# A transformer block pair on one core: normed rows turned by transposes, splits and chain steps moved in the middle

## The chip, the cores and the metric

The kernel runs on one core of one Trainium2 chip, in one launch. The metric is the device time of an execution in microseconds (us); the times given are medians of runs. Its engines are TensorE (PE in the rows; PEld is its weight load, which runs beside it), VectorE (DVE), ScalarE (ACT), GpSimd (POOL) and SyncE (SP), which only issues DMAs here. Each engine takes its instructions in the order in which the program wrote them.

## The reference

The input is x, 256 tokens of 1024 features, float32. Two blocks follow one another.

The first block: h = rmsnorm(x) times the projections q, k, v, g_attn, x_lru, g_lru; differential attention over 8 heads (two softmaxes, their difference times v, a norm per head, a gate); a causal convolution and a gated linear recurrence on x_lru; both halves go through w_out, and x = x + rmsnorm(y).

The second block: a = rmsnorm(x) times the projections of two mixers. The first (hg) is a gated linear attention in chunks of 64 tokens. The second (nsa) has 8 query heads on 2 key heads and adds three attentions: over compressed keys (blocks of 32 keys, stride 16, through a small two-layer network), over selected blocks and over a window; with 256 tokens all blocks are selected. Both go through w_out and are added to x. Then a routed layer (peer): rmsnorm(x) times wq, scores against two sets of 128 keys, the best 16 of 16 x 16 pairs per head, and for the chosen experts gelu(u . x) weighted into v. All 16384 rows of u and of v are read. At the end a gate: x + (p @ ple_proj) * sigmoid(rmsnorm(x) @ ple_gate). Cut to what matters here:

```
def rmsnorm(x, g):
    return x * rsqrt(mean(x * x, axis=-1, keepdims=True) + 1e-6) * g

a    = rmsnorm(x, mix_norm)            # second block, its three norms
h    = x + concat(hgrn2(a), nsa(a)) @ w_out
h    = h + peer(rmsnorm(h, ffn_norm))
out  = h + (p @ ple_proj) * sigmoid(rmsnorm(h, ple_gate_norm) @ ple_gate)
```

## The kernel before

**Products.** A float32 matrix product is done as three products of rounded parts: every weight and every activation is split into a high part (a rounded copy) and a low part (the rest), and `three` (L294) adds high x high, high x low and low x high in PSUM. A weight unit is 128 x 1024 numbers. `Units` (L45) holds the order of all units: SyncE loads a unit into one of four raw buffers (L67), ScalarE copies the high part (L83), VectorE subtracts for the low part (L89; GpSimd does a share in some stages, L87). `ensure(m)` issues the splits up to unit m, but not past `U.limit`; `take` hands out a unit and looks two units ahead. A unit of class "s" gets one of three stream buffers, one of class "h" one of seven hold buffers, and a split waits until the products with the buffer's former unit are done. A raw buffer's next load waits for the low part.

**Order.** All orders are written by the program itself: each engine runs what was issued to it, in that order. The long chains (attention heads, norms, recurrences) are Python generators. `tick` (L259) adds 1.3 to a virtual clock and steps those that are due; a generator that yields 2.6 is stepped again two ticks later. Products call `tick` after every twelve products of 256 columns (`feat_unit`, L299) or six of 512. So a yield says how many products PE gets between one step of a chain and the next. It is no time of the chip.

**Stages around the change.** In `attention_head` (L622) scores, softmax, transposes of the weights (L666), their copy wT (L669) and the products with v (L675) follow one another; `head_pair_out` (L680) norms and gates two heads (ya, L701) and transposes them (L708). The eight units of g_lru and the first units of w_out run beside the last heads.

Then come the output products of the first block (`split_tokens`, L790): the last six units of w_out ("h") are run through for token half 0 and then for token half 1, so all six stay in hold buffers. Beside the products of half 1, half 0 goes through `post_chain` (L768: square sums, root, gain, sum with x) and `norm_chain` (L403). The norm squares its rows on ScalarE, takes the root with seven small VectorE operations, and multiplies a 128 x 128 identity by it (`diagonal`, L382). `turn` (L387) takes eight blocks of 128 x 128 of the rows as stationary operand and the diagonal as moving one, so that each product scales and transposes a block; ScalarE (L397) then evacuates the high parts and VectorE (L400) the low parts, with the gain. `after_o1` (L888) steps these chains and, in half 1, raises `U.limit` by one unit after each product. The query and key units (nq, nk; six, all "h") follow in the same way: half 0, `turn` of half 1, half 1, with `nsa_norm` (L949: square sums, reduction qss, root, qn, transposes L971) beside them.

In the second block's mixers, `compress` (L998), `forget_pair` (L1109: the scan G, then d1 and d2), `hgrn` (L1138), `nsa_cmp` (L1229) and `nsa_pair` (L1274) are such generators too; the first steps of nsa wait for the end of `compress`. Small products share four PSUM banks in turn (`sm_bank`, L137).

After w_out of the second block, `after_o2` (L1463) adds to x, squares, takes the root and the diagonal; `ffn_norm0` turns half 0, and half 1 is turned (L1519) after the small products of ple_proj, whose results ScalarE evacuates (L1515). The next products (wq, L1742) need both halves of x. `turn_ple` at the end uses `turn` with the plain identity.

Of the kernel before, what the change touches and what calls it, by code (L numbers as in the profile page):

```python
# [13 lines left out]
F32 = mybir.dt.float32  # L14
# [6 lines left out]
OP = mybir.AluOpType  # L21
# [83 lines left out]
def body(ctx: ExitStack, tc: tile.TileContext, I, out):  # L105
# [73 lines left out]
        U.add(("o1", k), I["w1_out"][k], cls="s" if n < 10 else "h")  # L179
    end1 = len(U.seq) - 6  # L180
    for u in range(4):
        U.add(("nq", u), I["w2_nq"][u], cls="h")
    for u in range(2):
        U.add(("nk", u), I["w2_nk"][u], cls="h")
    end1h = len(U.seq)
# [198 lines left out]
        nc.vector.tensor_scalar(dg, ident, r, None, op0=OP.mult)  # L384
        return dg

    def turn(tt, src, dg, x, gname, ks=range(KD)):  # L387

        lt = slice(tt * P, (tt + 1) * P)
        for k0 in range(ks[0], ks[-1] + 1, 2):  # L390
            pt = sm_bank("ps_n")
            for j in range(2):
                k = k0 + j
                nc.tensor.matmul(pt[:, j * P:(j + 1) * P], lhsT=src[:, tt, k * P:(k + 1) * P], rhs=dg, start=True, stop=True)
            for j in range(2):
                k = k0 + j
                nc.scalar.activation(x[0][:, k, lt], pt[:, j * P:(j + 1) * P], AF.Copy, scale=col(gname, k))  # L397
            for j in range(2):
                k = k0 + j
                nc.vector.scalar_tensor_tensor(x[1][:, k, lt], pt[:, j * P:(j + 1) * P], col(gname, k),  # L400
                                               x[0].bitcast(F32)[:, k, lt], op0=OP.mult, op1=OP.subtract)

    def norm_chain(tt, pool, gname, x, name, wait=0):  # L403

        ss = sums(name)
        for half in range(2):
            square_sum(ss, half, halves(res, tt)[half], pool)
        dg = diagonal(rsqrt_of_pair(ss, name), name)
        yield
        for _ in range(wait):  # L410
            yield
        turn(tt, res, dg, x, gname)


    U.limit = end1
# [206 lines left out]
    def attention_head(hd, pq, pair):  # L622

        yield 1.3
        qk = w1.tile([P, 2, T], F32, name="qk")
        nc.scalar.activation(qk, pq.rearrange("p (a b) -> p a b", b=T), AF.Copy)
        yield 2.6
        smx = w1.tile([P, 2, 384], F32, name="smx")
        mx = tiny.tile([P, 4], F32, name="mx")
        zs = tiny.tile([P, 4], F32, name="zs")  # L630
        pss = [sm_bank("ps_s0"), sm_bank("ps_s1")]
        for qb in range(2):
            kl = P * (qb + 1)
            for c in range(2):
                rows = slice(c * 64, c * 64 + 64)
                nc.tensor.matmul(pss[c][:, qb * P:qb * P + kl], lhsT=qk[rows, 0, qb * P:(qb + 1) * P],
                                 rhs=qk[rows, 1, :kl], start=True, stop=True)
        yield 1.3
        for qb in range(2):
            kl = P * (qb + 1)  # L640
            for c in range(2):
                nc.vector.tensor_tensor_reduce(smx[:, c, qb * P:qb * P + kl], pss[c][:, qb * P:qb * P + kl],
                                               causal[:, 256 - kl:], 1.0, NEG, OP.add, OP.max,
                                               accum_out=mx[:, 2 * c + qb:2 * c + qb + 1])
        nc.vector.tensor_scalar(mx, mx, -0.125, None, op0=OP.mult)
        yield 2.6
        for qb in range(2):
            kl = P * (qb + 1)
            for c in range(2):
                j = 2 * c + qb  # L650
                nc.scalar.activation(smx[:, c, qb * P:qb * P + kl], smx[:, c, qb * P:qb * P + kl], AF.Exp,
                                     bias=mx[:, j:j + 1], scale=0.125, accum_out=zs[:, j:j + 1])
        yield 2.6
        nc.vector.reciprocal(zs, zs)
        nc.vector.tensor_scalar(zs[:, 2:4], zs[:, 2:4], nlam, None, op0=OP.mult)
        wt = w1.tile([P, 384], F32, name="wt")
        for qb in range(2):
            kl = P * (qb + 1)
            cs = slice(qb * P, qb * P + kl)
            nc.vector.tensor_scalar(wt[:, cs], smx[:, 0, cs], zs[:, qb:qb + 1], None, op0=OP.mult)  # L660
            nc.vector.scalar_tensor_tensor(wt[:, cs], smx[:, 1, cs], zs[:, 2 + qb:3 + qb], wt[:, cs],
                                           op0=OP.mult, op1=OP.add)
        yield 2.6
        pt = sm_bank("ps_wt")
        for b in range(3):
            nc.tensor.transpose(pt[:, b * P:(b + 1) * P], wt[:, b * P:(b + 1) * P], ident)  # L666
        yield 1.3
        wT = w1.tile([P, 384], F32, name="wT")
        nc.scalar.activation(wT, pt[:, :384], AF.Copy)  # L669
        yield 1.3  # L670
        if not pair:
            pair.append(po_bank("ps_o"))
        po = pair[0][:, (hd % 2) * T:(hd % 2 + 1) * T]
        vc = slice(hd * P, (hd + 1) * P)
        nc.tensor.matmul(po[:, 0:P], lhsT=wT[:, 0:P], rhs=vt[:, 0, vc], start=True, stop=True)  # L675
        nc.tensor.matmul(po[:, P:2 * P], lhsT=wT[:, P:2 * P], rhs=vt[:, 0, vc], start=True, stop=False)
        nc.tensor.matmul(po[:, P:2 * P], lhsT=wT[:, 2 * P:3 * P], rhs=vt[:, 1, vc], start=False, stop=True)
        heads_done.append(hd)

    def head_pair_out(hp, pair):  # L680

        while not (2 * hp in heads_done and 2 * hp + 1 in heads_done):
            yield
        po = pair[0]
        sl = slice(2 * hp, 2 * hp + 2)
        osq = w1.tile([P, 512], F32, name="osq")
        nc.scalar.activation(osq, po, AF.Square)
        yield 1.3
        oss = tiny.tile([P, 4], F32, name="oss")
        nc.vector.tensor_reduce(oss, osq.rearrange("p (a b) -> p a b", b=P), axis=AX.X, op=OP.add)  # L690
        ors = rsqrt_of_sum(oss, 4, P, EPS, "or")
        yield 2.6
        while hp // 2 not in gates_rows:
            yield
        ya = w1.tile([P, NT, 2 * P], F32, name="ya")
        for j in range(2):
            hd = 2 * hp + j
            for qb in range(2):
                a = 2 * j + qb
                hs = slice(hd * P, (hd + 1) * P)  # L700
                nc.vector.scalar_tensor_tensor(ya[:, qb, j * P:(j + 1) * P], po[:, a * P:(a + 1) * P], ors[:, a:a + 1],  # L701
                                               gs[:, qb, hs], op0=OP.mult, op1=OP.mult)
        po_free.append(hp)
        yield 2.6
        py = sm_bank("ps_y")
        for j in range(2):
            for qb in range(2):
                nc.tensor.transpose(py[:, j * T + qb * P:j * T + (qb + 1) * P], ya[:, qb, j * P:(j + 1) * P], ident)  # L708
        yhv = flat(yh[:, sl])
        nc.scalar.activation(yhv, py, AF.Copy, scale=subg)  # L710
        yield 2.6
        nc.vector.scalar_tensor_tensor(flat(yl[:, sl]), py, subg, yhv.bitcast(F32), op0=OP.mult, op1=OP.subtract)
# [48 lines left out]
    hold_stack = rt.enter_context(ExitStack())  # L761
    hold = open_pool(hold_stack, "hold", 7, side="right")
    U.pools["h"] = (hold, 7, 2)
    U.limit = end1 + 7
    nrm = open_pool(hold_stack, "nrm2", side="right")
    pgb = nrm.tile([P, D], F32, name="post_g")
    nc.scalar.dma_start(pgb, I["post_g"].partition_broadcast(P))
# [120 lines left out]
    def after_o1(n, tt):  # L888
# [5 lines left out]
        else:  # L894
            if n == -1:
                next(ch[1])
            else:
                if n == 3:
                    finish(ch[0])
                if n == 5:  # L900
                    next(ch[1])
                if n == 0:
                    next(ch[0])
                U.limit += 1
                U.ensure(U.limit)

    split_tokens([("o1", k) for k in O1h],
# [13 lines left out]
    def after_nqk(n, tt):  # L921
        if tt == 0:
            if n == 0:
                next(ch[1])
            if n == 5:
                finish(ch[1])
                bq.append(po_bank("ps_nq"))
                bk.append(po_bank("ps_nk"))
                spawn(nsa_norm(0))
        else:  # L930
            tick()

    qT = b2.tile([P, 4, T], F32, name="qT")
# [64 lines left out]
    def compress(ps):  # L998
# [15 lines left out]
        for j in range(2):  # L1014
            for g in range(2):
                src = bass.AP(ksh.tensor, ksh[:, j, g, 0:1].offset, [list(ksh.ap[0]), [2, 16], [16, 15]])
                nc.vector.tensor_tensor(cinv[:, j, :, g, :], src, pec[:, j, :].unsqueeze(2).to_broadcast([P, 16, 15]), OP.add)
        yield 2.6
        h1T = cm.tile([64, 2, 2, 16], F32, name="h1T", bufs=1)
        nc.gpsimd.memset(h1T, 0.0)  # L1020
        yield from sm_wait(1)
# [87 lines left out]
    def forget_pair(np_, ps):  # L1109
# [7 lines left out]
        if np_ == 1:  # L1117
# [4 lines left out]
            nc.vector.tensor_tensor_scan(flat(G), flat(rst), flat(sg), 0.0, OP.mult, OP.add)  # L1122
            yield 2.6
            nc.vector.tensor_tensor(d1, G, G[:, :, 31:32].to_broadcast([P, 16, 64]), OP.subtract)
            nc.vector.tensor_tensor(d2, G[:, :, 63:64].to_broadcast([P, 16, 64]), G, OP.subtract)
            hg_ready["d"] = True

# [335 lines left out]
    def after_o2(half, tt):  # L1463
        add_half(res, tt, half, banks)
        square_sum(ss[tt], half, halves(res, tt)[half], w2, "osq2")
        if half:
            dgs[tt] = diagonal(rsqrt_of_pair(ss[tt], "n3%d" % tt), "n3")
            nc.scalar.dma_start(res_d[:, tt], res[:, tt])

    def ffn_norm0():  # L1470
# [1 line left out]
        after_o2(0, 0)  # L1472
        after_o2(1, 0)
        yield 6.5
        turn(0, res, dgs[0], x, "ffn")

    t_n0 = spawn(ffn_norm0())
    while not (1 in nsa_done and 1 in hg_done):
# [31 lines left out]
    for tt in range(NT):  # L1510
# [5 lines left out]
        nc.scalar.dma_start(pp_d[:, tt], pp[:, tt])  # L1516
        if tt == 0:
            U.ensure(U.done + 1)
    turn(1, res, dgs[1], x, "ffn")  # L1519
    pre.close()  # L1520


# [324 lines left out]
        U.ensure(U.done + 1)  # L1847

    def turn_ple(tt, half):
        turn(tt, res, ident, gT, "ple", range(4 * half, 4 * half + 4))  # L1850

    v_last(0, 0)
    v_last(0, 1)
# [113 lines left out]
```

## Time and profile before

| | us |
|---|---|
| median of 3 runs | 1233.61 (1228.92 to 1235.35) |
| the profiled execution's own time | 1229.46 |
| its span | 1227.7 |
| PE busy in the span | 1199.4 (98%) |
| VectorE busy | 914.7 (75%) |
| ScalarE busy | 632.6 (52%) |
| GpSimd busy | 149.8 (12%) |
| chain of work that ended last | PE 81%, VectorE 11%, ScalarE 4% |

The span is the profiled execution from its first to its last instruction; the own time is a little longer. PE's matmuls are pipelined and their ends are modelled, so a busy PE need not be at its peak. The first 100 us hold the first projections, 100 to 185 attention, 185 to 230 the first block's output, 230 to 405 the second block's mixers, and from 405 on the routed layer with its 256 units of u and v.

### The profile page before, as it was taken

How to read it: one execution, taken by the hardware profiler on the slowest of the kernel's cores; microseconds unless marked ns; L12 is line 12 of the kernel's file. 1: busy time of each engine (PE TensorE's matmuls, PEld its weight loads, DVE VectorE, ACT ScalarE, POOL GpSimd, SP SyncE). 2: the span in 40 equal slices, each digit the busy share in tenths (PEclk: the TensorE clock that was granted, in tenths of full speed). 3: DMA queues.
4: the chain of work that ended last, by engine and by line, in shares of the span. 5: the costliest groups of instructions: out<-in, count | busy, mean ns of one | idle time of the engine just before them, and what ended most of it. 6: DMA issues, size and time to landing. Idle time of an engine off the chain costs nothing.

```text
span 1227.7 us, 22587 instructions
## 1 busy us (share of the span) xinstructions
PE 1199.4 (98%) x8797; PEld 1081.2 (88%) x8797; DVE 914.7 (75%) x1964; ACT 632.6 (52%) x953; POOL 149.8 (12%) x231
## 2 busy tenths in 40 slices
PE   8999989899999999999999999999999999999998
PEld 8979988788887999999999999998888888888876
DVE  6799886758887689987887688788888555555544
ACT  6955665546664554545555444445444444444453
POOL 3410012000000577300000000000000000000061
PEclk9999999999999999999999999999999999999999
DMA  7464437353224756665555655555555675566561
GB/s 239 146 191 153 138 132 242 128 190 104 87 87 136 233 162 184 194 198 175 164 164 157 191 175 185 176 182 177 186 173 174 206 252 191 191 194 198 189 210 48
DMA packets 59083, 211.78 MB, mean 172 GB/s; under 512 B 6560, under 2 KB 7648, under 8 KB 58592
## 3 DMA queue, kind: packets, MB, share of 16 engines
q1 hardware_dynamic: 56736, 204.60, 52.5%
q10 hardware_dynamic: 2240, 5.75, 1.4%
q8 instruction: 69, 1.13, 0.4%
q14 instruction: 38, 0.31, 0.1%
HBM read 206.65 MB, written 3.15 MB: 171 GB/s over the span
## 4 chain that ended last, share of the span: by engine, by line
PE 81%; DVE 11%; ACT 4%; issue 2%; POOL 1%; DMA 1%; ACTq 0%; SPq 0%; DVEq 0%; POOLq 0%
PE ps_u L295 10%; PE ps_u L297 10%; PE ps_u L296 10%; PE ps_acc L295 9%; PE ps_acc L297 9%; PE ps_acc L296 9%; DVE los L89 3%; PE ps_w L1713 1%; PE ps_w L1714 1%; ACT his L83 1%; PE ps_pq L296 1%; PE ps_pq L297 1%; PE ps_pq L295 1%; PE ps_out L295 1%; PE ps_out L297 1%
## 5 line engine op out<-in xcount | busy, mean ns | idle before, releaser
L89 DVE TENSOR_TENSOR los<-raw,his 128x1024 fp32r<-128x1024 f32 (+2 forms) x351 | 406.1, 1160 | 232.5 <-ACT his L83 231.4
L83 ACT ACTIVATE his<-raw 128x1024 fp32r<-128x1024 f32 (+1 forms) x351 | 369.9, 1057 | 332.0 <-PE ps_acc L297 166.6
L295 PE MATMUL ps_u<-x,his 128*128 128x256 f32 x1024 | 288.2, 281 | 0.0
L297 PE MATMUL ps_u<-x,los 128*128 128x256 f32 x1024 | 283.7, 277 | 0.0
L296 PE MATMUL ps_u<-x,his 128*128 128x256 f32 x1024 | 283.5, 277 | 0.0
L295 PE MATMUL ps_acc<-his,c 128*128 128x512 f32 x496 | 194.4, 392 | 0.0
L296 PE MATMUL ps_acc<-los,c 128*128 128x512 f32 x496 | 193.1, 389 | 0.0
L297 PE MATMUL ps_acc<-his,c 128*128 128x512 f32 x496 | 193.1, 389 | 0.0
L295 PEld LDWEIGHTS ps_u<-x,his 128*128 128x128 f32 x1024 | 192.8, 188 | 0.0
L296 PEld LDWEIGHTS ps_u<-x,his 128*128 128x128 f32 x1024 | 192.4, 188 | 0.0
L297 PEld LDWEIGHTS ps_u<-x,los 128*128 128x128 f32 x1024 | 192.2, 188 | 0.0
L87 POOL TENSOR_TENSOR los<-raw,his 128x256 fp32r<-128x256 f32 (+1 forms) x102 | 78.9, 803 | 715.4 <-ACT his L83 714.8
L297 PEld LDWEIGHTS ps_acc<-his,c 128*128 128x128 f32 x496 | 93.1, 188 | 19.7
L296 PEld LDWEIGHTS ps_acc<-los,c 128*128 128x128 f32 x496 | 93.1, 188 | 18.9
L295 PEld LDWEIGHTS ps_acc<-his,c 128*128 128x128 f32 x496 | 93.1, 188 | 18.9
L1753 ACT ACTIVATE R<-ps_u 128x512 f32<-128x512 f32 x38 | 22.7, 598 | 64.9 <-PE ps_u L297 64.9
L1703 DVE TENSOR_TENSOR o<-iota,i1p 128x1024 f16<-128x1024 f16 x64 | 43.8, 685 | 0.0
L1755 ACT ACTIVATE ps_u<-ps_u 128x512 f32<-128x512 f32 x26 | 15.1, 582 | 52.6 <-PE ps_u L297 52.6
L89 DVE TENSOR_TENSOR loh<-raw,hih 128x1024 fp32r<-128x1024 f32 (+1 forms) x30 | 30.7, 1039 | 14.7 <-ACT hih L83 13.0
L1713 PE MATMUL ps_w<-o2h,o 128*128 128x52 f16 (+1 forms) x512 | 39.7, 192 | 0.0
L1714 PE MATMUL ps_w<-o2l,o 128*128 128x52 f16 (+1 forms) x512 | 39.1, 191 | 0.0
L1781 DVE TENSOR_TENSOR c<-R,c 128x1024 fp32r<-128x1024 f32 (+2 forms) x33 | 38.8, 1178 | 0.0
(579 smaller groups left out, 2303.7 us busy)
## 6 DMA issues: line engine op xcount, KB each, us to landing
raw<-u SPq DMA_DIRECT2D x128, 512.0 KB, 3.7
raw<-v SPq DMA_DIRECT2D x128, 512.0 KB, 3.5
raw<-w_out SPq DMA_DIRECT2D x24, 512.0 KB, 3.8
raw<-wq SPq DMA_DIRECT2D x16, 512.0 KB, 4.1
raw<-w_f SPq DMA_DIRECT2D x10, 512.0 KB, 4.3
raw<-w_xl SPq DMA_DIRECT2D x8, 512.0 KB, 5.5
raw<-w_v SPq DMA_DIRECT2D x8, 512.0 KB, 3.6
raw<-w_ga SPq DMA_DIRECT2D x8, 512.0 KB, 3.6
```

The lines of the kernel that those rows point to most:

```text
L83: nc.scalar.activation(hi[:, :n], raw[:, :n], AF.Copy)
L87: nc.gpsimd.tensor_tensor(lo[:, a:b], raw[:, a:b], hi.bitcast(F32)[:, a:b], OP.subtract)
L89: nc.vector.tensor_tensor(lo[:, :c], raw[:, :c], hi.bitcast(F32)[:, :c], OP.subtract)
L295: nc.tensor.matmul(ps, lhsT=lh, rhs=rh, start=start, stop=False)
L296: nc.tensor.matmul(ps, lhsT=lh, rhs=rl, start=False, stop=False)
L297: nc.tensor.matmul(ps, lhsT=ll, rhs=rh, start=False, stop=stop)
L1703: nc.vector.tensor_tensor(rows(o1, P), i1, pairs(i1p, tsl, P), OP.is_equal)
L1713: nc.tensor.matmul(pw[:, j], lhsT=o1[:, g0 + j], rhs=oh_[:, g0 + j, :n], start=True, stop=False)
L1714: nc.tensor.matmul(pw[:, j], lhsT=o1[:, g0 + j], rhs=ol_[:, g0 + j, :n], start=False, stop=True)
L1753: nc.scalar.activation(flat(R[0][:, 2 * ip:2 * ip + 2]), ps, AF.Gelu_apprx_tanh)
L1755: nc.scalar.activation(ps, ps, AF.Gelu_apprx_tanh)
L1781: nc.vector.tensor_tensor(flat(lo), flat(src), flat(hi.bitcast(F32)), OP.subtract)
```

## The change

1. `diagonal` and the product with it are replaced, in the three norms that use `turn` with a root (`norm_chain` for both token halves, `after_o2` for both): `scaled` multiplies the rows by the root, the first 512 columns on VectorE and the other 512 on ScalarE, and `turn` then transposes eight blocks with the PE's transpose. The buffers are those of the square sums. `turn_ple` at the end keeps the products with the identity, written out. The very first norm is not touched.
2. The first two of the four nq units go into the stream's buffers; the limit before the first block's last output products is nine units instead of seven; raising it stops at the end of nk. The two c units and the first nv unit are split after the nq/nk products of half 0, and of the first and third product of half 1.
3. Yields grow: wT to its use 1.3 to 2.6; ya to its transposes 2.6 to 3.9; compress ahead of its products 2.6 to 5.2; and d2 is put 3.9 behind d1.

```diff
-        U.add(("nq", u), I["w2_nq"][u], cls="h")
+        U.add(("nq", u), I["w2_nq"][u], cls="s" if u < 2 else "h")
...
+    def scaled(r, tt, pool, name, tag):
+        xs = [pool.tile([P, 512], F32, name=name + "x", tag=tag, bufs=2) for _ in range(2)]
+        nc.vector.tensor_scalar(xs[0], halves(res, tt)[0], r, None, op0=OP.mult)
+        nc.scalar.activation(xs[1], halves(res, tt)[1], AF.Copy, scale=r)
+        return xs
+
-    def turn(tt, src, dg, x, gname, ks=range(KD)):
+    def turn(tt, xs, x, gname):
...
-                nc.tensor.matmul(pt[:, j * P:(j + 1) * P], lhsT=src[:, tt, k * P:(k + 1) * P], rhs=dg, start=True, stop=True)
+                nc.tensor.transpose(pt[:, j * P:(j + 1) * P], xs[k // 4][:, k % 4 * P:(k % 4 + 1) * P], ident)
...
-        dg = diagonal(rsqrt_of_pair(ss, name), name)
+        xs = scaled(rsqrt_of_pair(ss, name), tt, pool, name, "junk")
...
         nc.scalar.activation(wT, pt[:, :384], AF.Copy)
-        yield 1.3
+        yield 2.6
...
         po_free.append(hp)
-        yield 2.6
+        yield 3.9
...
-    U.limit = end1 + 7
+    U.limit = end1 + 9
...
-                U.limit += 1
+                U.limit = min(U.limit + 1, end1h)
                 U.ensure(U.limit)
...
                 spawn(nsa_norm(0))
+                U.limit = end1h + 1
+                U.ensure(U.limit)
         else:
+            if n in (1, 3):
+                U.limit += 1
+                U.ensure(U.limit)
             tick()
...
                 nc.vector.tensor_tensor(cinv[:, j, :, g, :], src, pec[:, j, :].unsqueeze(2).to_broadcast([P, 16, 15]), OP.add)
-        yield 2.6
+        yield 5.2
...
             nc.vector.tensor_tensor(d1, G, G[:, :, 31:32].to_broadcast([P, 16, 64]), OP.subtract)
+            yield 3.9
             nc.vector.tensor_tensor(d2, G[:, :, 63:64].to_broadcast([P, 16, 64]), G, OP.subtract)
...
         if half:
-            dgs[tt] = diagonal(rsqrt_of_pair(ss[tt], "n3%d" % tt), "n3")
+            dgs[tt] = scaled(rsqrt_of_pair(ss[tt], "n3%d" % tt), tt, w2, "n3", "osq2")
             nc.scalar.dma_start(res_d[:, tt], res[:, tt])
...
-        turn(0, res, dgs[0], x, "ffn")
+        turn(0, dgs[0], x, "ffn")
...
-    turn(1, res, dgs[1], x, "ffn")
+    turn(1, dgs[1], x, "ffn")
```

## Rows read from the trace of the kernel before

**Rows 1.** Stretches: length, busy us of PE, PEld, DVE, ACT, POOL, clock, DMA.

```profile
220.00:240.00 20.00, 16.60 (x90) 13.56 (x88) 18.31 (x45) 11.90 (x26) 0.00 (x0) 1.00 0.42 127
240.00:260.00 20.00, 18.87 (x134) 17.39 (x134) 12.11 (x38) 9.17 (x23) 1.33 (x5) 1.00 0.34 116
...
460.00:500.00 40.00, 40.00 (x355) 40.00 (x354) 37.87 (x214) 19.41 (x23) 32.58 (x44) 1.00 0.62 185
```

**Rows 2.** PE's waits: line, what it waited for: us in total, times, longest.

```profile
PE ps_n L394 <- DVE n21d L384: 2.7, 1, 2.7
...
PE ps_ct L1260 <- DVE nmx L1290: 2.5, 2, 2.2
PE ps_y L708 <- DVE ya L701: 2.0, 2, 1.3
PE ps_o L675 <- ACT wT L669: 1.6, 3, 1.1
...
PE ps_n L394 <- DVE n3d L384: 1.1, 1, 1.1
...
PE ps_n L394 <- DVE n20d L384: 0.7, 1, 0.7
...
PE ps_n L394 <- ACT ig L1515: 0.5, 1, 0.5
...
PE ps_qT L971 <- DVE qn L962: 0.5, 1, 0.5
PE ps_nq L297 <- DVE a L400: 0.3, 1, 0.3
```

**Rows 3.** PE in order of time: start, length, instruction [idle before it].

```profile
228.43 0.40 PE L295 MATMUL ps_nq<-hih,a 128*128 128x512 f32 x1
228.67 0.39 PE L296 MATMUL ps_nq<-loh,a 128*128 128x512 f32 x1
...
240.35 2.05 PE L394 MATMUL ps_n<-n21d,res 128*128 128x128 f32 x16 [2.70 <-DVE n21d L384]
```

**Rows 4.** The chain of waits at the transposes of the mixed rows: start, length, what.

```profile
362.29 0.87 PE ps_mT L1430 x8
```

**Rows 5.** VectorE in order of time around the first norm, columns as in rows 3.

```profile
224.80 0.29 DVE L384 TENSOR_SCALAR n20d<-ident,n20z 128x128 f32<-128x128 f32 x1
225.00 3.49 DVE L89 TENSOR_TENSOR loh<-raw,hih 128x1024 fp32r<-128x1024 f32 x3
...
229.01 2.15 DVE L400 SCALAR_TENSOR_TENSOR a<-ps_n,smalls,a 128x128 fp32r<-128x128 f32 x8
231.08 2.35 DVE L89 TENSOR_TENSOR loh<-raw,hih 128x1024 fp32r<-128x1024 f32 x2
```

**Rows 6.** VectorE's groups by form: busy us, mean ns, idle before.

```profile
L1121 DVE TENSOR_SCALAR fg<-fg 128x1024 f32<-128x1024 f32 x1 | 0.7, 687 | 0.0
```

**Rows 7.** ScalarE in order of time around the last norm.

```profile
398.05 1.04 ACT L83 ACTIVATE his<-raw 128x1024 fp32r<-128x1024 f32 x1
399.00 1.06 ACT L1515 ACTIVATE ig<-ps_pp 128x512 f32<-128x512 f32 x2
...
402.90 2.18 ACT L397 ACTIVATE x<-ps_n,smalls 128x128 fp32r<-128x128 f32 x8 [0.41 <-PE ps_n L394]
```

**Rows 8.** ScalarE in order of time around the first norm.

```profile
222.87 2.94 ACT L83 ACTIVATE hih<-raw 128x1024 fp32r<-128x1024 f32 x3
...
226.28 2.16 ACT L397 ACTIVATE a<-ps_n,smalls 128x128 fp32r<-128x128 f32 x8
```

**Rows 9.** VectorE in order of time, the first query norm.

```profile
244.07 0.95 DVE L957 TENSOR_REDUCE qss<-qsq 128x12 f32<-128x768 f32 x1 [0.15 <-ACT qsq L954]
...
246.91 0.76 DVE L962 TENSOR_TENSOR qn<-ps_nq,qrz 128x256 f32<-128x256 f32 x2
```

**Rows 10.** Two stretches near the start, columns as in rows 1 (seventh: clock).

```profile
20.00:40.00 20.00, 18.10 (x139) 17.69 (x139) 15.95 (x26) 16.36 (x26) 12.47 (x27) 0.91 0.65 212
...
28.00:30.00 2.00, 2.00 (x11) 2.00 (x11) 1.02 (x2) 0.90 (x2) 1.67 (x4) 0.50 0.82 264
```

More of the change, by code (lines that the diff above doesn't have):

```diff
@@ L385, in diagonal @@
         return dg
-    def turn(tt, src, dg, x, gname, ks=range(KD)):
+    def scaled(r, tt, pool, name, tag):
[4 more added lines that the diff above has]
+    def turn(tt, xs, x, gname):
         lt = slice(tt * P, (tt + 1) * P)
-        for k0 in range(ks[0], ks[-1] + 1, 2):
+        for k0 in range(0, KD, 2):
             pt = sm_bank("ps_n")
@@ L411, in norm_chain @@
             yield
-        turn(tt, res, dg, x, gname)
+        turn(tt, xs, x, gname)
     U.limit = end1
@@ L1849, in turn_ple @@
     def turn_ple(tt, half):
-        turn(tt, res, ident, gT, "ple", range(4 * half, 4 * half + 4))
+        lt = slice(tt * P, (tt + 1) * P)
+        for k0 in range(4 * half, 4 * half + 4, 2):
+            pt = sm_bank("ps_n")
+            for j in range(2):
+                nc.tensor.matmul(pt[:, j * P:(j + 1) * P], lhsT=res[:, tt, (k0 + j) * P:(k0 + j + 1) * P], rhs=ident,
+                                 start=True, stop=True)
+            for j in range(2):
+                nc.scalar.activation(gT[0][:, k0 + j, lt], pt[:, j * P:(j + 1) * P], AF.Copy, scale=col("ple", k0 + j))
+            for j in range(2):
+                nc.vector.scalar_tensor_tensor(gT[1][:, k0 + j, lt], pt[:, j * P:(j + 1) * P], col("ple", k0 + j),
+                                               gT[0].bitcast(F32)[:, k0 + j, lt], op0=OP.mult, op1=OP.subtract)
     v_last(0, 0)
```

## The prediction

> **What bounds the kernel now.** I read the stretches (windows) first: there the reader sees TensorE (PE) busy without a break in 460 to 500 us, but only 16.6 of 20 us in 220 to 240 [rows 1]. So what is lost in the middle (about 100 to 405 us) reaches the end one for one, and what the other engines do counts only where PE waits for it. PE's waits come next, and they show which chain ends last at each of these places [rows 2]; nine of its groups, 11.9 us together, are what the change can touch. Last I read the engine timelines around the longest waits, to see what is queued behind what.
>
> The sum is made against the profiled execution: span 1227.7 us, its own time 1229.46. The median of the runs before, 1233.61, lies 4.15 above that, and the forecast is moved by as much.
>
> **The change part by part.**
>
> *More products between a chain's steps (attention).* PE waits three times for wT (1.6 in all) and twice for ya (2.0) [rows 2]. The transposed weights' use moves one tick later, the transposes of ya two ticks later while ya itself moves one, so each place gains one tick. A tick is six products of 512 columns (or twelve of 256), which start 0.24 apart, so 1.4 us [rows 3], more than the longest of these waits (1.1 and 1.3). Nothing is added to any queue; the head pairs finish a tick later, and the three units of output products behind them cover that. I take -3.6; bounds -3.6 and 0 (ScalarE's copy of wT could shift along).
>
> *Transposes for products with a diagonal.* Eight blocks by products with the diagonal are 16 PE instructions, 2.05 us [rows 3]; eight true transposes of the same size take 0.87 [rows 4]. That is -1.18 in each of four turns, -4.7 in all, but only where nothing else is late behind a turn.
>
> *Two scaled halves for the diagonal.* The diagonal took VectorE 0.29 for 128 columns [rows 5]; 1024 columns of the nearest form take 0.69 [rows 6]. For 512 I take 0.45 (bounds 0.29 and 0.69), so the first transposes start 0.16 later. The second half is a ScalarE copy of 512 columns; two copies of that size take 1.06 [rows 7], so 0.53 to 0.65. The wait that this adds: ScalarE now stands still until VectorE has the root. Queued behind it are the splits of weights and, behind those, the evacuation of the very blocks that are being turned.
>
> *First norm, token half 0 (225 us).* Before, ScalarE used the 1.9 us of the root's arithmetic (222.9 to 224.8) for three splits, 0.98 each, and reached the evacuation at 226.28 [rows 8]. After, the scaled half ends near 225.45, and four splits stand before the evacuation instead of three: the limit is now nine units, eight are split by then, the first product of token half 1 asks for two more and the next two for one each. 4 x 0.95 + the square sum 0.6 put the evacuation at 229.85, 3.6 later. VectorE's four low parts, each gated by its high part, end at 231.05 (before: three, from 225.00, 3.49 long), the half of yg at 231.7, where its own evacuation begins; before that was 229.01 [rows 5]. PE: turn 225.35 to 226.25, six output products, ready for nq at 227.6; it needs the low parts at 232.0. Stall 4.0 instead of 0.3 (bounds 0.3, if the splits don't get in the way, and 4.5).
>
> *Token half 1 (240 us).* From the first evacuation of half 0 (229.01) to the next turn (240.35) were 11.3 us of VectorE's chain, with two low parts of 2.35 inside [rows 3, 5]; those two are done earlier now, and so is a third that held the root up by about 0.25. So the turn could start at 231.7 + 11.3 - 2.6 = 240.4 with a diagonal, and 0.2 to 0.4 later with the scaled half, near 240.8. PE ends the nq and nk products at 240.3 (8.2 us after 232.0, as before), so it waits 0.5 instead of 2.7. Sum of both halves: +0.2 (start of the turn) + 3.7 - 2.2 - 2 x 1.18 = -0.65. The splits were to leave the chain; most of what leaves it comes back one stage earlier.
>
> *Three units split ahead, under the nq products of half 1.* The high and low parts of c0 and c1 are issued ahead of the query norm's reduction. That began at 244.07, right behind VectorE's evacuation, and its end (qn) is at 247.6 [rows 9]. Two low parts of 1.16 and 0.65 of waiting for ScalarE (a square sum lies between the two high parts) and the shift of the chain put qn at 251.1; PE, 0.7 early, asks for it at 248.5. A new stall of 2.5 (bounds 0 and 3.0). In exchange the 0.5 of the second qn goes [rows 2], and some 0.3 of a product that waited for a low part in c. Their DMAs are no worse off: each load waits for a raw buffer, and these come free earlier. Sum +1.7.
>
> *compress, d2.* The block compression moves two ticks, and with it every step of nsa; d2 moves three ticks, to the tick in which the last query rows are ready, so hgrn starts no later. The transposes of the compressed scores waited 2.2 of the 2.5 for a bank that VectorE reads [rows 2], behind G, d1, d2 and a low part. Both the bank's reader and the user move two ticks, VectorE's work in that stretch stays the same and full, and d2 now stands just ahead of the same reader. I take -0.3; bounds -2.2 and +1.5.
>
> *Last norm.* Half 0: the turn ends 1.0 earlier, but what follows hangs on ScalarE's and VectorE's chain to the second root (the n3d wait, 1.1 [rows 2]), so nothing is won. Half 1: before, ScalarE filled the root's arithmetic with a split from 398.05 and two evacuations, and after one more of each began on x at 402.90, 4.85 later, of which it idled 0.41 [rows 7]. After, the scaled half stands ahead of all these and ends at 400.7 (the root is there by 400.0): x from 400.7 + 4.4 = 405.1, 2.2 later, or 1.7 if the other short pauses in there go too, and the first products of the next stage with it. The DMA that saves the rows is issued from ScalarE behind the scaled half, about 2 us later, and is read back only in the last stage. I take +1.7; bounds -1.2 (only the shorter turn counts) and +2.2.
>
> Total: -3.6 - 0.65 + 1.7 - 0.3 + 1.7 = **-1.1**, that is 1228.4 for an execution like the profiled one and **1232.5** on the scale of the median.
>
> [...]
>
> **The rivals.**
>
> 1. *The chains get short, as the moved splits suggest.* ScalarE's wait then finds cover and no split stands before an evacuation. Then the waits for a (0.3) and n21d (2.7) go, two turns are worth 2.4, qn 0.5, ct 2.2, the last norm 1.1 + 0.5 + 1.2, attention 3.6: -14.5, 1219; half of that, 1226. For it: VectorE is busy only 12.1 of the 20 us from 240 to 260 [rows 1]. Against it: the orders counted above, since ScalarE and VectorE take their work in order.
>
> 2. *The clock falls* (slower than before). Place: the three new stalls. The fall before cost 20 x (1 - 0.91) = 1.8 us [rows 10]. Three of them are +5.4, less 0.5 that the wait before the second turn takes up: 1232.5 + 4.9 = 1237.4; with falls twice as long, 1242. It decides if stalls like the new ones let the granted clock fall, as in rows 10 and unlike the wait in rows 2.
>
> 3. *The transposes are no cheaper than the products* (the change doesn't do what it says there): the two turns that count give back 2.4, 1234.9. Against it: 16 instructions against 8 [rows 3, 4].
>
> **How the numbers follow.** Forecast 0.62, rival 1 0.16, rival 2 0.17, rival 3 0.05. 0.5% is 6.2 us, about what a measurement of this kernel tells from no change. Faster by more needs -6.2: rival 1 beyond its halfway point and a corner of the forecast, 0.17. Slower by more: the longer falls of rival 2 and the upper bounds together, 0.12. Within: 0.71. The range runs from halfway into rival 1 (1226) to the middle of rival 2 (1240).
>
> **What would show it.** Right: no wait over 0.3 for wT and ya; a turn of 8 instructions in 0.9; ScalarE idle about 1.9 before each scaled half; a PE stall of 3 to 4 us in the first nq products and one over 2 for the first qn; x evacuated 1.5 to 2 later after the last pp product. Wrong: if PE goes through nq without a stall, the order of the splits was misread and rival 1 holds; if the attention waits stay, -3.6 falls away; a granted clock under 1.00 between 225 and 410 is rival 2.

## The result: 12.7 us slower, and the profile after

The changed kernel took 1246.94 us (median of 4 runs, 1243.59 to 1247.86), the kernel before 1234.22 beside it; ratio 1.0118, 95% interval 1.0096 to 1.014. The forecast was 1232.5, with a range that ended at 1240. Run again on another chip it came to 1.0102 (1.0083 to 1.0121). The two profiled executions lie further apart, 1227.7 and 1245.7 us of span, because that of before was one of its quickest. Of these 18.0 us PE was idle in 13.5 (41.8 against 28.3 over the span) and busy in 4.5, although four turns of eight transposes need some 4 less than before (1.06 for 2.05 each).

PE's waits between 100 and 430 us of the changed kernel (columns as in [rows 2]):

```profile
PE ps_n L401 <- ACT ig L1528: 4.8, 2, 3.6
PE ps_wt L673 <- DVE wt L668: 4.3, 5, 2.5
PE ps_mT L1443 <- DVE ohg L1235: 3.5, 1, 3.5
PE ps_nq L295 <- ACT a L404: 2.4, 1, 2.4
PE ps_qT L983 <- DVE qn L974: 1.8, 1, 1.8
PE ps_mT L1443 <- DVE on L1369: 1.6, 1, 1.6
PE ps_cs L1250 <- ACT kcT L1084: 1.5, 1, 1.5
```

Beside [rows 2] the reader sees that the four longest of the waits that the change was to touch are gone (n21d, ct, ya, wT), and that larger ones, for other things, stand in their place. In the kernel before none of the seven was over 0.5.

The clock is the second difference. Stretches of the changed kernel (columns as in [rows 1]; the number after the busy times is the granted clock):

```profile
165.00:170.00 5.00, 2.04 (x14) 1.66 (x13) 4.89 (x13) 3.01 (x4) 1.52 (x1) 0.95 0.30 106
170.00:175.00 5.00, 5.00 (x34) 5.00 (x33) 2.88 (x4) 1.74 (x4) 0.07 (x1) 0.71 0.55 184
230.00:235.00 5.00, 3.31 (x7) 2.21 (x8) 5.00 (x12) 3.39 (x13) 0.00 (x0) 0.59 0.90 297
235.00:240.00 5.00, 5.00 (x17) 3.94 (x17) 3.80 (x14) 1.39 (x4) 0.00 (x0) 0.73 0.16 65
295.00:300.00 5.00, 5.00 (x34) 4.86 (x33) 4.16 (x7) 2.09 (x4) 0.00 (x0) 0.66 0.19 66
365.00:370.00 5.00, 3.96 (x15) 3.05 (x16) 4.18 (x20) 3.42 (x11) 0.00 (x0) 0.74 0.16 66
410.00:415.00 5.00, 1.17 (x4) 0.57 (x4) 2.55 (x6) 3.56 (x5) 0.00 (x0) 0.68 0.46 188
415.00:420.00 5.00, 4.18 (x16) 3.29 (x17) 3.52 (x10) 3.28 (x11) 0.00 (x0) 0.50 1.00 356
```

In the kernel before, the granted clock was 1.00 in all of them. Here it falls behind five waits of 1.5 to 3.6 us, as low as 0.50 in 415 to 420 (in an execution of this kernel on another chip, s2_after below, it stayed at 1.00 in 295 to 300, behind the same wait of 1.5 for kcT). In 5 us at 0.59 it withheld 5 x 0.41 = 2 us. Over a whole run this withheld clock, (1 - mean granted clock) x span, is 15.2 us (mean of 4 runs) against 4.4 (27 runs of before, on another chip). It is no price yet, since part of it lies in time in which PE stood idle (in 410 to 415, at 0.68, PE was busy for 1.17 of 5): of the 12.2 us that the eight stretches withheld, 9.5 fall on PE's busy time (an estimate: each stretch's withheld time, times the share of it in which PE was busy).

The last norm shows how one wait hands the next its start. ScalarE of the changed kernel, in order of time (start, length, instruction, idle before it):

```profile
408.42 0.63 ACT L371 ACTIVATE junk<-res 128x512 f32<-128x512 f32 x1 [1.95 <-DVE res L791]
...
411.04 0.72 ACT L391 ACTIVATE n3x<-res,n31z 128x512 f32<-128x512 f32 x1 [1.89 <-DVE n31z L340]
411.05 0.33 ACTq L1481 DMA_DIRECT2D res_d<-res  x1
411.66 1.04 ACT L83 ACTIVATE his<-raw 128x1024 fp32r<-128x1024 f32 x1
412.61 1.06 ACT L1528 ACTIVATE ig<-ps_pp 128x512 f32<-128x512 f32 x2
...
415.04 1.06 ACT L1528 ACTIVATE ig<-ps_pp 128x512 f32<-128x512 f32 x2
...
416.51 2.17 ACT L404 ACTIVATE x<-ps_n,smalls 128x128 fp32r<-128x128 f32 x8 [0.40 <-PE ps_n L401]
```

And PE at the same place:

```profile
409.29 0.40 PE L297 MATMUL ps_pp<-hih,php 128*128 128x512 f32 x1
413.24 1.17 PE L401 MATMUL ps_n<-ident,n3x 128*128 128x128 f32 x4 [3.56 <-ACT ig L1528]
415.67 1.18 PE L401 MATMUL ps_n<-ident,n3x 128*128 128x128 f32 x4 [1.26 <-ACT ig L1528]
416.93 0.58 PE L295 MATMUL ps_pq<-x,his 128*128 128x256 f32 x1
```

In [rows 7] ScalarE did the split and the first pp evacuation (399.00) while VectorE worked out the root. Here it stands 1.89 for the root, and the scaled half, the split and the evacuation follow one after another. PE does not wait for the scaled rows: it waits for `ig`, the reader of the pp banks, because the transposes take their banks from the same ring of four. From the last pp product (ends 409.69; before 399.37) to the first pq product are 7.24 us instead of 3.95.

### The profile page after: what moved, and what is told of

Read it like the earlier page. It is cut to its first block, busy times and chain, and to the rows that moved or that the text cites. A ratio compares the mean times of both kernels' runs of the same rounds, so it can differ in the third digit from the quotient of the medians.

```text
span 1245.7 us, 22531 instructions
## 1 busy us (share of the span) xinstructions
PE 1203.9 (97%) x8765; PEld 1083.0 (87%) x8765; DVE 916.4 (74%) x1964; ACT 634.6 (51%) x957; POOL 151.3 (12%) x231
## 4 chain that ended last, share of the span: by engine, by line
PE 79%; DVE 11%; ACT 5%; issue 2%; DMA 1%; POOL 1%; ACTq 0%; DVEq 0%; POOLq 0%
PE ps_u L295 10%; PE ps_u L296 9%; PE ps_u L297 9%; PE ps_acc L295 9%; PE ps_acc L297 9%; PE ps_acc L296 9%; DVE los L89 3%; ACT his L83 2%; PE ps_w L1726 1%; PE ps_pq L296 1%; PE ps_pq L297 1%; PE ps_w L1727 1%; PE ps_pq L295 1%; PE ps_out L296 1%; PE ps_out L297 1%
## 5 line engine op out<-in xcount | busy, mean ns | idle before, releaser
L89 DVE TENSOR_TENSOR los<-raw,his 128x1024 fp32r<-128x1024 f32 (+1 forms) x353 | 407.6, 1157 | 233.6 <-ACT his L83 230.8
L83 ACT ACTIVATE his<-raw 128x1024 fp32r<-128x1024 f32 x353 | 372.3, 1058 | 325.9 <-PE ps_acc L297 167.5
```

The lines of the kernel that those rows point to most:

```text
L83: nc.scalar.activation(hi[:, :n], raw[:, :n], AF.Copy)
L89: nc.vector.tensor_tensor(lo[:, :c], raw[:, :c], hi.bitcast(F32)[:, :c], OP.subtract)
```

## The experiments

**The four parts, each alone on the kernel before.** Their edits, shortened:

```diff
# p1_attention
-        yield 1.3              # ahead of wT's use
+        yield 2.6
-        yield 2.6              # ahead of ya's transposes
+        yield 3.9
# p2_turns: scaled() for diagonal(), transposes for products, all four turns
-        dg = diagonal(rsqrt_of_pair(ss, name), name)
+        xs = scaled(rsqrt_of_pair(ss, name), tt, pool, name, "junk")
# p3_limits
-    U.limit = end1 + 7
+    U.limit = end1 + 9         # and class "s" for nq 0, 1; the three other limits
# p4_compress
-        yield 2.6              # compress
+        yield 5.2
+            yield 3.9          # ahead of d2
```

> The kernel before with the attention's part alone (wT used a tick later, ya turned a tick later than it was). Theory F (a PE stall of about 2.5 us or more lets the granted clock fall, and the fall costs 1.5 to 3 us beyond the stall): the waits for wT and ya (3.6) go, a wait of 2.5 for wt comes near 166 us with a clock under 1.00 behind it; +0.5 to +1.5 us, about 1235. Rival S (only the length of a stall counts): 3.6 less, 4.3 more, +0.7 without a fall of the clock. The prediction's term would be -3.6, about 1230.6.

> The kernel before with the scaled halves and true transposes alone, in all four turns; the order of the weight splits is as before. Theory F: the waits before the last turn grow to 3.5 and more, the clock falls behind them, and the last norm alone costs 4 to 6 us; the first norms give back about 1; net +3 to +5, about 1238. Rival S: the last norm costs 2 to 3 (stall only), the first norms give back 1: +1 to +2, about 1235.7. The prediction's terms: +1.7 for the last norm and -2.4 for two turns: 1233.5.

> The kernel before with only the two value units in the stream's buffers and the limits that go with them. Theory F: four splits stand ahead of the first evacuation, PE stalls about 3 in the first nq products and 1.8 before qT, the clock falls near 230 us for about 3.4 us of loss, the wait of 2.7 before the second turn goes: net +3 to +4, about 1237.5. Rival S: stalls alone 4.8 - 3.2, +1.5, 1235.7, clock at 1.00 throughout. A third, that the splits' order is not what delays the evacuation but the scaled half is: no stall at nq, -1 to -3.

> The kernel before with the block compression two ticks later and d2 three ticks later, nothing else. Theory M (the two mixers end later, where no products stand behind them): the wait of 2.2 for ct goes, but waits of 3 to 4 for ohg and 1 to 2 for on come before the output products, nsa's last products stand inside them, and the clock falls near 365 us: +5 to +8, about 1240.5. Rival: the late end of the mixers comes from the later start of the stage (the query norm's stall), not from this part: then this run is within 1 of before (the prediction's term is -0.3).

| run | median, us | ratio to before (95%) | clock withheld, us |
|---|---|---|---|
| before, same chip | 1232.16 | | 4.4 |
| p1_attention | 1233.90 | 1.0023 (1.0004 to 1.0041) | 7.3 |
| p2_turns | 1240.62 | 1.0069 (1.0043 to 1.0094) | 10.5 |
| p3_limits | 1229.55 | 0.9982 (0.9961 to 1.0003) | 2.1 |
| p4_compress | 1239.19 | 1.0063 (1.0045 to 1.0080) | 5.1 |

So the loss has two main makers, the turns and the compression; the limits gain a little, if anything. p1's waits are those that Theory F named (4.3 for wt), with a time between its 1235 and the 1232 of before; but its trace also has a wait of 2.3 for `cin`, which this edit does not touch and the trace of before does not have, so not all of its loss need be the attention's. p3 refutes Theory F's figure and Rival S's: stalls of 1.5 and 1.4 come (nq, qT), the one of 2.7 goes, and the clock withheld over the whole run is 2.1, less than before. Its time is that of the third theory, whose mark, no stall at nq, did not come. p4 settles for Theory M, and its withheld clock is only 0.7 above that of before, so nearly all of its loss is the waiting itself. The ratios add to 1.0137, against 1.0118 and 1.0102 for the whole; p2 carries a wait of 3.1 for `cin` that the whole does not have (r1 below).

p4's place of loss, on PE (first fence) and VectorE (second):

```profile
359.50 1.09 PE L1322 MATMUL ps_pt<-ident,es 128*128 128x128 f32 x8
364.08 1.10 PE L1431 MATMUL ps_mT<-ident,ohg 128*128 128x128 f32 x4 [3.48 <-DVE ohg L1223]
...
367.92 2.45 PE L1339 MATMUL ps_no<-vv,eT 128*128 128x128 f32 x16
```

```profile
357.32 1.14 DVE L1309 TENSOR_SCALAR es<-es,nzs 128x256 f32<-128x256 f32 x4
358.38 0.41 DVE L1291 CUSTOM_DVE_ANT_0 es<-ps_ns,ald 128x256 f32<-128x256 f32 x1
...
359.95 1.23 DVE L89 TENSOR_TENSOR loh<-raw,hih 128x1024 fp32r<-128x1024 f32 x1
361.09 0.68 DVE L1219 TENSOR_REDUCE hss<-osq 128x4 f32<-128x512 f32 x1
...
363.67 1.13 DVE L1223 SCALAR_TENSOR_TENSOR ohg<-ps_ho,hrz,ig 128x128 f32<-128x128 f32 x4
```

The same place in the kernel before, PE:

```profile
357.01 2.05 PE L1338 MATMUL ps_no<-vv,eT 128*128 128x128 f32 x16
358.89 1.04 PE L1321 MATMUL ps_pt<-ident,es 128*128 128x128 f32 x8
360.24 2.05 PE L1338 MATMUL ps_no<-vv,eT 128*128 128x128 f32 x16 [0.31 <-ACT eT L1328]
362.13 0.60 PE L1430 MATMUL ps_mT<-ident,ohg 128*128 128x128 f32 x4
```

Before, two of nsa's groups and their transposes (2.05 + 1.04 + 2.05) covered hgrn's normalisation on VectorE. Two ticks later they stand behind the first output products, only the eight transposes (1.09) are left as cover, and VectorE has nsa's scaling, scores and a low part ahead of `hss`. `ohg` ends 3.0 later, PE waits 3.48 for it and 1.7 for `on` later. The waits for ct (2.2 of [rows 2]) go; 1.5 for kcT and 0.9 twice for low parts come.

**ScalarE or the scaling itself? The clock or the stall? Compression or d2? And a first combination.**

```diff
# q1_vector: p2_turns, and
-        nc.scalar.activation(xs[1], halves(res, tt)[1], AF.Copy, scale=r)
+        nc.vector.tensor_scalar(xs[1], halves(res, tt)[1], r, None, op0=OP.mult)
# q2_fill: p2_turns, and in turn(), last turn alone
+            for n in range({0: 26, 4: 10}.get(k0, 0)):
+                nc.tensor.matmul(fill[:, :P], lhsT=ident, rhs=ident, start=True, stop=True)
# q3_compress_only: p4_compress without d2's yield
# q4_combined: p3_limits, q1_vector and ya's "yield 3.9"
```

> As p2_turns (turns alone), but VectorE scales both halves, so ScalarE waits for no root. Theory A (ScalarE, in order, stands still for the root, and the split and the two evacuations of pp behind it come late, whose banks the last transposes want): the wait of 3.8 before the last turn falls to about 1.6 for the scaled half and 0.5 for ig, no fall of the clock there, 8 of the 8.5 us of p2_turns come back: about 1231.5 (1230 to 1233). Rival B (scaling 1024 columns instead of making a diagonal of 128 is itself too long for the chain): still over 1236.

> As p2_turns, with products of 128 columns that nobody reads put into PE's two waits of the last turn (26 ahead of the first transpose, 10 ahead of the fifth), so PE is busy while ScalarE is as late as before. Theory F (the fall of the clock costs beyond the stall): ScalarE's evacuations keep their times, the granted clock stays at 1.00 from 405 to 420 and the time falls by 3 to 4 us from 1240.6 to about 1237. Rival S (only the stall counts): 1240.6, within 1.

> The kernel before with the block compression two ticks later; d2 as it was. Theory M (the compression's delay alone puts two of nsa's groups behind the last products, where the mixers' end is uncovered): 1239, within 1.5, with the waits of 3.5 for ohg and 1.7 for on. Rival D (d2's new place ahead of the reader of the bank is the cost): within 1.5 of before, 1232.

> The limits and the two value units of the change, its transposes with both halves scaled by VectorE, and of the attention only the later transposes of ya; compression and d2 as before. If the parts add: limits -2.6, turns -0.5 to -1, the two waits for ya -2.0: about 1227 (1225.5 to 1229). Rival: the splits that the limits put ahead of an evacuation collide with VectorE's longer scaling: a stall over 2 in the first nq products and no gain, 1231 or more.

Measured: q1 1234.73, ratio 1.0018 (1.0005 to 1.0032); q2 1237.37, 1.0048 (1.0031 to 1.0066); q3 1242.05, 1.0071 (1.0053 to 1.0089); q4 1230.63, 0.9984 (0.9972 to 0.9996). q1 gives back most of p2's loss, as Theory A said: PE's wait before the last turn is now 1.9 for VectorE's scaled half, and only 0.4 is left for ig. It stays slower than before: what the transposes save (8 in 1.06 for 16 in 2.05), the scaling of 1024 columns takes back (n3x 1.9, n3d before 1.1), and `cin` costs 2.9 in its trace. q2 leans to Theory F, 2.6 us less by the ratios with ScalarE as late as before, though its interval overlaps p2's. q3: the compression alone makes the loss, 3 us above Theory M's figure (its trace has one more wait, 1.7 for scT); d2 adds nothing that shows. q4 came near the time of its rival, with the stall in the first nq products (2.8) that the rival named.

**Undoing the compression in the changed kernel; filling a wait of before; two combinations.**

```diff
# r1_no_compress: the changed kernel, and
-        yield 5.2
+        yield 2.6
-            yield 3.9          # ahead of d2
# r2_before_fill: the kernel before, in turn() for token half 1 of the first norm
+                for n in range(20):
+                    nc.tensor.matmul(pt[:, :P], lhsT=ident, rhs=ident, start=True, stop=True)
# r3_limits_ya: p3_limits and ya's "yield 3.9"
# r4_combined_fill: q4_combined and such products: 20 ahead of nq, 14 and 5 in the last turn
```

> The changed kernel with the block compression and d2 back where they were. If the parts add (Theory M): 7.5 to 8.5 us less than the changed kernel, a ratio to before of about 1.005 (1238.5), waits for ohg and on gone, ct's 2.2 back. Rival C (the delay also covers the landing of the shifted copy, for which PE waited 3 us in the runs with the turns alone): that wait of 3 appears, with a fall of the clock, and only 3 to 4 come back, a ratio of 1.008.

> The kernel before with 20 products of 128 columns that nobody reads in PE's wait of 2.7 for the second diagonal. Theory F (that wait lets the clock fall in some executions and not in others, and this is part of the scatter of the runs): the granted clock's mean rises, and the median falls by 1 to 2 us while the lowest time stays near 1228. Rival S: no change of either.

> The change's limits and two value units, and the later transposes of ya; diagonals, compression, d2 and wT as before. If the two add: limits -2.2 to -2.6, the waits for ya (2.0) replaced by about 1.7 of waits for wt and a low part, so -0.3: about 1229.5, ratio 0.9978. Rival: the later ya is worth its 2.0: 1227.5.

> As q4_combined, with products that nobody reads in PE's waits before the first nq products (20), before the last turn (14) and inside it (5). Theory F: the falls of the clock at 230 and 400 us go (1.7 each), nothing else moves: 1227.5, ratio 0.996. Rival S: as q4_combined, 0.9984, or 0.5 worse where the products outlast the waits.

Measured: r1 1240.37, 1.0065 (1.0043 to 1.0088); r2 1231.85, 0.9996 (0.9984 to 1.0007); r3 1229.69, 0.9975 (0.9962 to 0.9988); r4 1230.04, 0.9981 (0.9969 to 0.9994). r1 lies between its two theories. The wait of rival C is there, 1.9 us for `cin`, which needs the copy shifted by DMA; it was 3.1 in p2_turns and is absent from the changed kernel, so the longer way for the compression does hide that landing. (The turns are not what makes this wait: the traces of p1, s4 below and r2, which have no scaled half, show it with 2.3, 1.9 and 1.3.) The cost of the compression inside the change is then 4.6 to 6.5 us (1.0102 or 1.0118 less 1.0065, of 1233) rather than the 7.8 it costs alone. r2 shows no gain from filling a single wait of 2.7: withheld clock fell from 3.6 to 2.5, the time did not follow. r4 shows none over q4 either. (In both, the filling products outlast the waits; see s1 below.) r3, which came as its parts add, has the lowest ratio of all and is faster than both kernels; the intervals of p3, q4 and r4 overlap its own.

**How much is the clock? And which edit makes the wait for wt?**

```diff
# s1_after_fill: the changed kernel, with products nobody reads (128 columns)
+        18 into pt ahead of the last head's weight transposes
+        20 into bq[0] ahead of the first nq product
+        26 into pt ahead of mix_T(0, 0)
+        26 and 10 in the last turn, as in q2_fill
# s2_after: the changed kernel as it is
# s3_after_vector: the changed kernel with q1_vector's edit
# s4_wT_only: the kernel before with wT's "yield 2.6"
```

> The changed kernel with products of 128 columns that nobody reads in four of PE's waits: 18 before the last head's weight transposes, 20 before the first nq products, 26 before the first transposes of the mixers' outputs, 26 and 10 in the last turn. Theory F (the falls of the clock that these waits bring lengthen the work behind them): the granted clock stays at 1.00 at 170, 230 to 240, 365 to 375 and 410 to 425 us; by the low clock in time that PE was busy there, 1.5 + 2.7 + 1.5 + 3.5, up to 9 us less than s2_after, about 1238; at half of that 1242. Rival S (the stalls alone make the loss, and the falls lie inside them): within 1.5 of s2_after.

> The changed kernel unaltered, on the chip of the three others, as their base: 1245 to 1248 by either theory.

> The changed kernel with both halves scaled by VectorE, so that ScalarE waits for no root. Theory A (ScalarE in order): the wait before the last turn falls from 3.6 to about 1.9 and the one for the first a from 2.4 + 0.6 to about 2.8 for VectorE's part; 4 to 6 us less than s2_after, as q1_vector against p2_turns (5.9), about 1241.5. Rival: the first norm's new stall stays, the turn's is replaced by the later scaled half: 1 to 2 less.

> The kernel before with the use of wT one tick later, ya's transposes as before. Theory W (a head that ends a tick later puts ya's root, 2.7 of VectorE's time, and ya ahead of the next head's weights): the wait of 2.5 for wt near 166 us is there and the waits for wT are gone: +0.2 to +0.3% as p1_attention, 1235. Rival Y (ya's later transposes make it): no wait over 0.6 for wt, 1231 to 1232.

| run | median, us | ratio to before (95%) | clock withheld, us |
|---|---|---|---|
| s1_after_fill | 1241.45 | 1.0081 (1.0060 to 1.0101) | 2.3 |
| s2_after | 1245.17 | 1.0102 (1.0083 to 1.0121) | 14.7 |
| s3_after_vector | 1243.09 | 1.0084 (1.0060 to 1.0108) | 13.4 |
| s4_wT_only | 1232.48 | 0.9997 (0.9981 to 1.0012) | 5.2 |

In s1 the stretches that had fallen run at full clock:

```profile
230.00:235.00 5.00, 5.00 (x30) 4.33 (x29) 4.82 (x17) 1.73 (x7) 0.00 (x0) 1.00 0.74 266
...
410.00:415.00 5.00, 5.00 (x48) 5.00 (x47) 2.88 (x6) 3.46 (x9) 0.00 (x0) 1.00 0.79 270
415.00:420.00 5.00, 5.00 (x47) 5.00 (x46) 1.69 (x6) 2.15 (x5) 0.60 (x1) 1.00 0.78 254
```

Of 12.4 us of withheld clock given back, the time got 3.7 by the medians and 2.6 by the ratios, whose intervals overlap: a fifth to a third of the loss, less than Theory F's low figure (half of 9) and more than Rival S allows (1.5). Part of the low clock lay where PE had nothing to do, as in 410 to 415 above, busy 1.17 of 5. But that part is small (2.7 of the 12.2 above), and the filling products outlast the waits. PE of s1 at two of the four places:

```profile
358.58 5.97 PE L1449 MATMUL ps_mT<-ident 128*128 128x128 f32 x52
364.39 0.60 PE L1455 MATMUL ps_mT<-ident,ohg 128*128 128x128 f32 x4
...
406.05 5.97 PE L400 MATMUL ps_fill<-ident 128*128 128x128 f32 x52
411.86 0.60 PE L404 MATMUL ps_n<-ident,n3x 128*128 128x128 f32 x4
```

In s2 PE takes up `ohg` 0.41 after VectorE has begun it (366.06, 366.47). In s1 VectorE begins it at 361.81, and PE is with the filling products until 364.39: 2.2 too late. At the last turn PE of s2 starts 0.63 behind the first `ig` (414.01, 414.64), PE of s1 2.69 behind it (409.17, 411.86): 2.1 too late. For wt and nq the same reckoning gives 0.6 and 0.5. So the filling took some 5 us of PE's time beyond the waits (an estimate), and 2.6 to 3.7 is the least that the clock cost here, not its price. With the 9.5 above, an estimate, as the most, its share of the loss (12.6 by s2's ratio) stays open between 2.6 and some 9 us. The other filled runs have the same flaw: their products outlast the waits by 1.8 and 2.1 (q2), 1.6 (r2), 1.5 and 1.0 (r4).

s3 refutes Theory A's size inside the change: 2.1 less, as its rival said. The last turn's wait fell from 3.56 to 1.93, but the first norm's did not shrink (2.8 for VectorE's `a`), and the clock still fell at both (0.68 in 230 to 235, 0.54 in 415 to 420). s4 speaks for Rival Y, in time and wait, yet its sense is not that ya makes the wait. With one of the two edits and not the other (s4 for wT; q4 and r3, beside their other parts, for ya) PE's longest wait for wt near 168 us is 0.6, with both 2.5. PE at this head in the kernel before, and then in p1_attention:

```profile
164.95 0.49 PE L675 MATMUL ps_o<-vt,wT 128*128 128x128 f32 x2 [1.06 <-ACT wT L669]
...
167.99 1.11 PE L708 MATMUL ps_y<-ident,ya 128*128 128x128 f32 x4 [0.72 <-DVE ya L701]
...
170.32 0.60 PE L666 MATMUL ps_wt<-ident,wt 128*128 128x128 f32 x3
```

```profile
166.71 0.39 PE L677 MATMUL ps_o<-vt,wT 128*128 128x128 f32 x2
...
170.99 0.33 PE L666 MATMUL ps_wt<-ident,wt 128*128 128x128 f32 x1 [2.51 <-DVE wt L661]
```

VectorE at the same place, in the kernel before and then in p1_attention:

```profile
167.59 1.12 DVE L701 SCALAR_TENSOR_TENSOR ya<-ps_o,orz,gs 128x128 f32<-128x128 f32 x4
...
169.28 0.35 DVE L661 SCALAR_TENSOR_TENSOR wt<-smx,zs,wt 128x128 f32<-128x128 f32 x1
```

```profile
168.88 1.12 DVE L701 SCALAR_TENSOR_TENSOR ya<-ps_o,orz,gs 128x128 f32<-128x128 f32 x4
...
170.58 0.35 DVE L661 SCALAR_TENSOR_TENSOR wt<-smx,zs,wt 128x128 f32<-128x128 f32 x1
```

VectorE is busy 4.69 and 4.83 of 5 us in 160 to 170 of the kernel before; there it works through ya's root, low parts, ya and wt in order, and wt is ready when that is done. The waits for wT and ya and ya's transposes only spent PE's time until then. Taken out of the way, they come back as one longer wait for wt. In the changed kernel the clock falls behind it (0.71 in 170 to 175), but that fall does not hang on the one long wait: s4, whose waits at this place are 0.7, 0.6 and 0.5, has it too:

```profile
170.00:175.00 5.00, 4.95 (x31) 4.95 (x32) 4.22 (x5) 1.88 (x4) 1.54 (x1) 0.70 0.36 119
```

## Why the prediction was wrong, step by step

**Compression (-0.3; alone +7.8, in the change 4.6 to 6.5).** The step that failed most: "Both the bank's reader and the user move two ticks, VectorE's work in that stretch stays the same and full". I followed the moved steps to the wait that they were to remove and not to the end of their own chain. There is no product behind the last tick of the mixers, so two ticks at the start are two uncovered ticks at the end: 3.5 and 1.7 of waits (p4) for the 2.2 that went.

**Attention (-3.6; alone +2.8 by the ratio, 1.7 by the medians, the wait for `cin` in it).** I let each wait vanish because a tick is longer than it. One of the two edits alone left the time where it was (s4 0.9997; r3 0.9975 against p3 0.9982). The term would hold if the waits had been ScalarE's or PE's lateness; the engine that bound the stretch was VectorE, busy 4.69 and 4.83 of 5 us, and both edits leave its work as it was.

**Last norm (+1.7; +3.3 to the first pq product).** ScalarE's wait for the root was forecast at 1.9 and measured 1.89; the delay behind it, with bounds that ended at +2.2, was mis-sized. What I left out is that the transposes' banks hang on the pp evacuations, which stand behind the scaled half and a split. I carried the delay to x's evacuation alone. VectorE had the root first, and keeping both halves on it was quicker, by 6 us for the turns alone (1.0069 against 1.0018) and by 2 in the whole change (1.0102 against 1.0084, where the intervals overlap).

**First norm and the splits (-0.65 and +1.7).** The mechanism held in the changed kernel: the four splits ahead of the evacuation, seen as

```profile
225.66 0.72 ACT L391 ACTIVATE n20x<-res,n20z 128x512 f32<-128x512 f32 x1 [1.90 <-DVE n20z L340]
226.29 3.88 ACT L83 ACTIVATE hih<-raw 128x1024 fp32r<-128x1024 f32 x4
...
230.65 2.16 ACT L404 ACTIVATE a<-ps_n,smalls 128x128 fp32r<-128x128 f32 x8
```

with a stall of 2.4 + 0.6 in the first nq products (forecast 4.0), none before the second turn (0.5), and 1.8 for the first qn (2.5). Either part alone makes some of that first stall: the splits 1.5 (p3), the scaled half 1.5 + 0.9 (p2). The transposes are 1.06 for 8 against 2.05, so rival 3 is out. The forecast 0.87 is a piece of the chain of waits in [rows 4]; on PE the same eight take 1.04 (362.13 to 363.17). What they save does not reach q1's time (1.0018), whose trace also holds the wait of 2.9 for `cin`.

**Rival 2** came in its first step: behind the new stalls the granted clock went to 0.50 to 0.74. But a fall did not come behind every wait, nor behind waits of that length alone: the one of 2.70 in the kernel before was followed by 1.00, and s4's clock fell to 0.70 with no wait over 0.7 beside it. The price of the falls (4.9 forecast) is not settled: by the estimates above at least 2.6, at most some 9. What the range lacked whatever that price is: stalls in seven places where I had put three, none of mine in the attention or at the end of the mixers. At the latter, waiting alone made most of 7.8 us (p4).

**Rival 1** holds nowhere as a whole; its sound core is p3 and r3. r3 keeps the limits and the later ya: PE waits 2.2 for ct, 1.8 for wT, 1.5 for nq's `a`, and none over 0.7 for n20d, ya or n21d.

What stays open: how the loss divides between the stalls and the low clock behind them; whether a single wait of 2 to 2.7 costs anything by the clock (r2 and r4 saw no gain, to about 0.15%, with products that outlast the waits); and why the shifted copy lands 5.2 us after its issue in the kernel before and 7.1 in s4 (medians), whose edit does not touch it. That its landing decides the wait for `cin` is seen (s4: VectorE waits 2.4 for the copy, and PE then 1.9 for `cin`); what delays it was not tried.

## What to carry to other kernels

A wait of PE names the engine that was late, not how much time is to be had: before moving PE's work past it, see whether that engine is busy without a break up to that point, since then the wait only moves and may grow (here 1.06 and 0.72 became 2.51). A chain started later ends later (here `ohg`, by 3.0), so follow it to its last step and ask what covers that. Work given to an engine that runs in order, behind a value another engine has yet to make, delays everything queued behind it, also the readers that free shared banks (here ScalarE's 1.89 for the root, and PE's 3.56 for `ig` behind it). And who fills a wait to learn what the clock behind it costs must fill no longer than it lasts (here products of 5.97 stood in a wait of 3.5).

## What the runs showed of the hardware

- The same kind of wait is not followed by the same clock: in the kernel before the granted clock stayed 1.00 behind the wait of 2.7 us near 238 us and fell to 0.50 in 28 to 30 us [rows 10], behind waits of 1.14 and 0.76. Behind the wait of 1.5 near 295 us of the changed kernel it fell to 0.66 in one execution and stayed 1.00 in another, and in s4_wT_only it fell to 0.70 in 170 to 175 us with no wait over 0.7 beside it.
- Giving back 12.4 us of withheld clock made the run 2.6 to 3.7 us shorter, while the filling products took some 5 us of PE's time beyond the waits (an estimate): withheld clock is no price, and its price was bounded here, not measured.
- The DMAs of the shifted copy (`ksh`) took 5.1 to 6.1 us from issue to landing in the kernel before, 5.9 to 6.9 in the changed kernel and 6.1 to 7.9 in s4_wT_only, whose edit does not touch them.
